# Eighteen gated pairs by seven block products, and state outputs as column halves

## The chip, the cores and the metric

The kernel runs on one core of a Trainium2 chip, as one launch. The metric is device time in microseconds (us), less is better; the time of a kernel is the median of its runs. Engines are named as in the profile: PE (TensorE, matmuls) with PEld (its weight loads), DVE (VectorE), ACT (ScalarE), POOL (GpSimd) and SP (SyncE, which issues most DMAs).

## What is computed

The kernel is a two-layer encoder trunk on 512 positions of width 1024, in float32. Layer 0 mixes positions by gated linear attention and a second recurrent mixer, layer 1 by retention and a diagonal complex state space (S5). After each mixer stands a gated feed-forward with a width-3 convolution over the positions:

```python
def conv_ffn(h, w_up, conv_w, conv_b, w_down):      # h: (1, 512, 1024), normed
    u = jnp.einsum('bsd,df->bsf', h, w_up)          # w_up: 1024 x 5632
    ...
    c = conv_b + up[:, 0:s] * conv_w[0]             # up: u padded by one position
    for t in range(1, CONV_WIDTH):
        c = c + up[:, t:t + s] * conv_w[t]
    a, v = jnp.split(c, 2, axis=-1)                 # 2816 columns each
    return jnp.einsum('bsf,fd->bsd', jax.nn.silu(a) * v, w_down)
...
x = x + conv_ffn(rmsnorm(x, g), ...)
```

The S5 part of layer 1 turns its states into outputs by matmuls with the real and the imaginary part of a matrix and a skip term.

## The kernel before, in words

Activations lie transposed: channels on the 128 partitions, the 512 positions along the free axis, so x is eight tiles of 128 x 512. Matmuls keep float32 precision by splitting both operands into a high part (a rounded copy, by ACT) and a low part (the rest, by DVE): `load_split` (L182, L184) does it for a weight chunk of 128 x 1024, `norm_split` for the activations. A product is then three matmuls, high x high, high x low, low x high (`mm3`). All matmuls go through the helper `mm`, so all have line L192.

The feed-forward (`ffn`) has 22 gated pairs. Pair m is two column blocks of 128, the gate m and the value m + 22. `up` makes each block from a weight chunk, with 8 x 3 matmuls of 512 columns (tile `pu`). `up_evac` scales the two results by the norm factor (`upad`, L306), convolves them (ACT starts `c` at L310, DVE adds two taps at L313), applies SiLU (`sa`, L318), multiplies (`g`, L320) and splits the product into `gh` (ACT, L323) and `gl` (DVE, L324). `down` multiplies a round of gated tiles by a down chunk into `pd` and adds the result to one tile of x (L346). ROUNDS sets three rounds of 8, 7 and 7 pairs: after the pairs of a round (and one more) come eight down products, one for each tile of x. The last three down products of the second feed-forward are made in column halves of 256 (`last`, tile `pl`), so that the final norm of the first half starts early.

The order of the work is set by a small scheduler in the program (`Sched`): it takes matmul jobs in the order of a list (`ffn_jobs`), issues the weight loads of the next three chunks ahead, and lets side chains advance when a clock of estimated matmul time has passed (the numbers in `W`). Each engine then runs its instructions in the order in which they stand; semaphores make the engines wait for each other. Weight chunks go through four raw buffers and four buffers each for the high and the low part.

In the S5 part, `states` makes the states' inputs `px` in column halves (two matmuls with 64 weight columns each, into partitions 0 to 63 and 64 to 127), and `outputs` makes `py` with three matmuls over 128 weight columns for each of four groups. It does so four times.

Of the kernel before, what the change touches and what calls it, by code (L numbers as in the profile page):

```python
# [11 lines left out]
F32 = mybir.dt.float32  # L12
F32R = mybir.dt.float32r
I32 = mybir.dt.int32
AF = mybir.ActivationFunctionType
# [28 lines left out]
ROUNDS = [list(range(0, 8)), list(range(8, 15)), list(range(15, 22))]  # L44
# [92 lines left out]
class Net:  # L137
# [33 lines left out]
    def load_raw(self, src, shape, name):  # L171
        n = int(np.prod(shape))
        raw = self.wp.tile([128, 1024], F32, tag="wraw", name=f"r_{name}", bufs=4)
        self.nc.sync.dma_start(out=raw[:, 0:n], in_=src)
        return raw, shape, name

    def load_split(self, raw, shape, name):
        nc = self.nc
        n = int(np.prod(shape))
        hi = self.wp.tile([128, 1024], F32R, tag="whi", name=f"h_{name}", bufs=4)  # L180
        lo = self.wp.tile([128, 1024], F32R, tag="wlo", name=f"l_{name}", bufs=4)
# [6 lines left out]
    def chunk(self, src, shape, name):  # L188
        return self.load_split(*self.load_raw(src, shape, name))

# [90 lines left out]
    def ffn(self, L, env, x, nxt, side=None, tail=None):  # L281
# [3 lines left out]
        with ExitStack() as st:  # L285
# [4 lines left out]
            gh, gl = {}, {}  # L290
            upad = []
            for i in range(4):
                u = fq.tile([128, S + 2], F32, tag=f"upad{i}", name=f"upad{L}_{i}")
                nc.gpsimd.memset(u[:, 0:1], 0.0)
                nc.gpsimd.memset(u[:, S + 1 : S + 2], 0.0)
                upad.append(u)
# [4 lines left out]
            def up_evac(m, pss):  # L301
                cs = []
                for half in range(2):
                    j = m + MF * half
                    u = upad[(2 * m + half) % 4]
                    nc.vector.tensor_tensor(  # L306
                        out=u[:, 1 : S + 1], in0=pss[half], in1=self.rbc, op=ALU.mult)
# [11 lines left out]
                g = fq.tile([128, S], F32, tag="g", name=f"g{L}_{m}", bufs=2)  # L319
                nc.vector.tensor_tensor(out=g, in0=sa, in1=cs[1], op=ALU.mult)  # L320
                h = fp.tile([128, S], F32R, tag="gh", name=f"gh{L}_{m}", bufs=9)
                l = fp.tile([128, S], F32R, tag="gl", name=f"gl{L}_{m}", bufs=9)
                nc.scalar.activation(h, g, AF.Copy)  # L323
                nc.vector.tensor_tensor(out=l, in0=g, in1=h.bitcast(F32), op=ALU.subtract)  # L324
                gh[m], gl[m] = h, l

# [8 lines left out]
            def down(r, ks, *chs):  # L335
                ms = ROUNDS[r]
# [8 lines left out]
                for k, ps in zip(ks, pd):  # L345
                    nc.vector.tensor_tensor(out=x[k], in0=ps, in1=x[k], op=ALU.add)  # L346
                    if r == len(ROUNDS) - 1:
                        nxt(k, x[k])

            def last(ks, *chs):  # L350
                ms = ROUNDS[-1]
# [13 lines left out]
            env.update(up=up, down=down, last=last)  # L365
# [6 lines left out]
    def ffn_jobs(self, L):  # L372
# [8 lines left out]
        done = -1  # L381
        for r, ms in enumerate(ROUNDS):
            upto = min(ms[-1] + 1, MF - 1)
            for m in range(done + 1, upto + 1):
                up(m)
            done = upto
            groups = [[k] for k in range(KD)]
            if r == len(ROUNDS) - 1:
                groups[0:2] = [[0, 1]]
                if L:  # L390
                    groups[-3:] = [[5, 6, 7]]
            for ks in groups:
                J(lambda *chs, r=r, ks=ks: env["down"](r, ks, *chs) if len(ks) < 3 else env["last"](ks, *chs),
                  [(self.I[f"w_down{L}_{r}"][k], (len(ms), 128), f"d{L}_{r}_{k}") for k in ks])
# [699 lines left out]
    def odd(self, env):  # L1094
# [50 lines left out]
        def s5():  # L1145
# [61 lines left out]
            def outputs(Q):  # L1207
                w1, w2, w0, E, H4 = st_.pop(Q)
# [248 lines left out]
    def start(self, warm):  # L1457
# [8 lines left out]
        raw += [self.wp.tile([128, 1024], F32, tag="wraw", name=f"r_qk{i}", bufs=4) for i in range(2)]  # L1466
# [227 lines left out]
```

## Time and profile before

| | |
|---|---|
| three runs, median | 1243.82 us (1243.2 to 1245.39) |
| the profiled execution, its own time | 1242.25 us |
| its span, first to last instruction | 1240.3 us |
| busy: PE / PEld | 99% / 82% |
| busy: DVE / ACT / POOL | 67% / 40% / 16% |
| mean granted TensorE clock | 0.996 of full speed |
| DMA | 133 MB, mean 107 GB/s |

Busy shares are averages over stages with different limits. The chain of waits follows the work that ended last back from the end: at each step to what released it, or to the instruction before it on its engine. A start in a timeline minus the start before it is the time that an instruction occupies its engine; the duration is a little longer, since neighbours overlap. "Idle before" is what an engine waited ahead of an instruction, with the one that released it.

### The profile page before, as it was taken

What the parts mean: (1) busy time and instruction counts of PE and PEld (TensorE: products, weight loads), DVE (VectorE), ACT (ScalarE), POOL (GpSimd) and SP (SyncE); (2) the same over time, 40 slices, a digit from 0 to 9 for tenths busy, and PEclk for the clock granted to TensorE, in tenths of its full rate; (3) what the DMA queues carried; (4) which work ended last, traced back from release to release, by engine and by line L of the source; (5) the groups of instructions that cost most, each with busy time, mean ns of one, the idle gap of its engine ahead of it and who ended that gap; (6) DMA issues with size and microseconds to landing.
All of it is one profiled execution on the core that took longest, in us unless ns stands there. A gap on an engine that the chain in (4) does not pass through costs nothing.

```text
span 1240.3 us, 19118 instructions
## 1 busy us (share of the span) xinstructions
PE 1224.3 (99%) x7675; PEld 1019.1 (82%) x7675; DVE 836.8 (67%) x1315; ACT 497.0 (40%) x659; POOL 195.4 (16%) x279
## 2 busy tenths in 40 slices
PE   9999999999999999999999998999999999999997
PEld 7788878888888888888889897888888888888886
DVE  6668766569985688567657866756677547745753
ACT  6545344344443444244433244325444224423442
POOL 1000001050084463500122320003000000000012
PEclk9999999999999999999999999999999999999999
DMA  7132132232316234342456533123233222233211
GB/s 246 49 104 69 36 121 86 78 127 86 98 39 192 88 121 143 123 159 71 153 169 203 166 98 125 62 85 119 86 102 102 87 101 100 83 107 102 91 45 68
DMA packets 54504, 133.01 MB, mean 107 GB/s; under 512 B 12432, under 2 KB 17936, under 8 KB 54416
## 3 DMA queue, kind: packets, MB, share of 16 engines
q1 hardware_dynamic: 53696, 131.25, 32.0%
q8 instruction: 60, 0.98, 0.3%
q10 hardware_dynamic: 720, 0.55, 0.1%
q14 instruction: 28, 0.23, 0.1%
HBM read 120.24 MB, written 11.53 MB: 106 GB/s over the span
## 4 chain that ended last, share of the span: by engine, by line
PE 94%; DVE 3%; issue 1%; POOL 1%; ACT 0%; DMA 0%; POOLq 0%; SPq 0%; DVEq 0%; ACTq 0%
PE pu L192 39%; PE pd L192 18%; PE wo L192 6%; PE v L192 4%; PE p_g L192 4%; PE sc L192 2%; PE ov L192 2%; PE p_q L192 2%; PE p_k L192 2%; PE p_hz L192 2%; PE p_rg L192 2%; PE pl L192 1%; PE rv L192 1%; PE o L192 1%; PE p_hq L192 1%
## 5 line engine op out<-in xcount | busy, mean ns | idle before, releaser
L192 PE MATMUL pu<-xh_f,h_u 128*128 128x512 f32 x704 | 275.2, 391 | 0.0
L192 PE MATMUL pu<-xh_f,l_u 128*128 128x512 f32 x704 | 274.1, 389 | 0.0
L192 PE MATMUL pu<-xl_f,h_u 128*128 128x512 f32 x704 | 274.1, 389 | 0.0
L192 PEld LDWEIGHTS pu<-xh_f,h_u 128*128 128x128 f32 x704 | 132.2, 188 | 28.3 <-issue 1.2
L192 PEld LDWEIGHTS pu<-xh_f,l_u 128*128 128x128 f32 x704 | 132.1, 188 | 27.8
L192 PEld LDWEIGHTS pu<-xl_f,h_u 128*128 128x128 f32 x704 | 132.2, 188 | 27.1
L182 ACT ACTIVATE h_u<-r_u 128x1024 fp32r<-128x1024 f32 x88 | 93.1, 1058 | 117.3 <-PE pd L192 52.8
L313 DVE SCALAR_TENSOR_TENSOR c<-upad,convp,c 128x512 f32<-128x512 f32 x176 | 133.5, 760 | 3.8 <-ACT c L310 1.0
L192 PE MATMUL pd<-gh,h_d 128*128 128x512 f32 x331 | 129.3, 391 | 0.0
L192 PE MATMUL pd<-gh,l_d 128*128 128x512 f32 x331 | 128.9, 389 | 0.0
L192 PE MATMUL pd<-gl,h_d 128*128 128x512 f32 x331 | 128.9, 389 | 0.0
L184 DVE TENSOR_TENSOR l_u<-r_u,h_u 128x1024 fp32r<-128x1024 f32 x88 | 108.8, 1236 | 16.2 <-ACT h_u L182 15.6
L306 DVE TENSOR_TENSOR upad<-pu,rstd_f 128x512 f32<-128x512 f32 x88 | 60.5, 688 | 71.1 <-PE pu L192 69.5
L346 DVE TENSOR_TENSOR x<-pd,x 128x512 f32<-128x512 f32 x45 | 31.0, 690 | 90.3 <-PE pd L192 90.3
L310 ACT ACTIVATE c<-upad,convp 128x512 f32<-128x512 f32 x88 | 71.3, 811 | 20.0 <-DVE upad L306 17.2
L323 ACT ACTIVATE gh<-g 128x512 fp32r<-128x512 f32 x44 | 27.8, 632 | 113.8 <-DVE g L320 113.8
L192 PEld LDWEIGHTS pd<-gh,l_d 128*128 128x128 f32 x331 | 62.1, 188 | 13.1
L192 PEld LDWEIGHTS pd<-gh,h_d 128*128 128x128 f32 x331 | 62.1, 188 | 13.1 <-issue 0.4
L192 PEld LDWEIGHTS pd<-gl,h_d 128*128 128x128 f32 x331 | 62.2, 188 | 12.8
L182 ACT ACTIVATE h_d<-r_d 128x896 fp32r<-128x896 f32 (+1 forms) x48 | 47.2, 987 | 63.4 <-PE pd L192 42.2
L318 ACT ACTIVATE sa<-c 128x512 f32<-128x512 f32 x44 | 27.8, 632 | 81.1 <-DVE c L313 81.1
L184 DVE TENSOR_TENSOR l_d<-r_d,h_d 128x896 fp32r<-128x896 f32 (+1 forms) x48 | 55.0, 1147 | 6.6 <-ACT h_d L182 4.4
(418 smaller groups left out, 2273.9 us busy)
## 6 DMA issues: line engine op xcount, KB each, us to landing
r_u<-in_w_up SPq DMA_DIRECT2D x88, 512.0 KB, 3.5
r_d<-in_w_down SPq DMA_DIRECT2D x32, 448.0 KB, 3.4
r_wo<-in_w_out SPq DMA_DIRECT2D x16, 512.0 KB, 3.4
r_d<-in_w_down SPq DMA_DIRECT2D x16, 512.0 KB, 3.5
w<-dw SPq DMA_DIRECT2D x20, 256.0 KB, 4.9
r_v<-in_we_v SPq DMA_DIRECT2D x8, 512.0 KB, 3.8
r_g<-in_we_g SPq DMA_DIRECT2D x8, 512.0 KB, 3.8
r_ov<-in_wo_v SPq DMA_DIRECT2D x8, 384.0 KB, 3.6
```

The lines of the kernel that those rows point to most:

```text
L182: nc.scalar.activation(hi[:, 0:n], raw[:, 0:n], AF.Copy)
L184: eng.tensor_tensor(out=lo[:, 0:n], in0=raw[:, 0:n], in1=hi[:, 0:n].bitcast(F32), op=ALU.subtract)
L192: self.nc.tensor.matmul(ps, a, b, start=start, stop=stop)
L306: nc.vector.tensor_tensor(out=u[:, 1 : S + 1], in0=pss[half], in1=self.rbc, op=ALU.mult)
L310: nc.scalar.activation(c, u[:, 1 : S + 1], AF.Identity, scale=cw[:, 1:2], bias=cw[:, 3:4])
L313: nc.vector.scalar_tensor_tensor(out=c, in0=u[:, o : o + S], scalar=cw[:, tap : tap + 1], in1=c, op0=ALU.mult, op1=ALU.add)
L318: nc.scalar.activation(sa, cs[0], AF.Silu)
L323: nc.scalar.activation(h, g, AF.Copy)
L346: nc.vector.tensor_tensor(out=x[k], in0=ps, in1=x[k], op=ALU.add)
```

## The change

Pairs 4 to 21 of the second feed-forward (18 of 22) are made by Strassen's scheme in its form with seven products. For a pair the weights are seen as two by two blocks: gate and value columns by the upper and the lower half of the input channels. The activations are two by two as well: lower and upper half of the channels by the first and the second 256 positions. Seven block products of 128 columns by 512 channels by 256 positions replace eight.

- `right` makes the seven right operands once, from the normed activations (tiles `bh`, `bl`, four of 128 x 1792 each): DVE normalises, POOL forms four differences, ACT and DVE split. It waits for the norm factor.
- `block_loads` makes the weight side of a pair: the two loaded chunks, two chunks of sums and differences (tiles `ws`, four 512-wide additions on POOL), and the splits: `ua`, `us`, `ut` of 1024 columns and `ug` of 512.
- `blocks` runs the products, two in a PSUM tile `pb`, and puts them together in `upad` by five additions on DVE, two copies on ACT and one addition on POOL (on DVE for the last pair). `gated` is the rest of the old evacuation; the product `g` now overwrites `sa`.
- The rounds of the second feed-forward become 4 ordinary pairs and 6, 6 and 6 changed ones, and the eight down products of a round are put between the blocks of the next round, four for every three pairs. `gh` and `gl` of most changed pairs take over the buffers of the normed activations.
- Raw, high and low weight buffers go from four to five, and loads are issued four chunks ahead in the second feed-forward.
- `py` is made in column halves: six matmuls with 64 weight columns for each group.

The diff, cut to its core:

```diff
+M0 = 4
+cut = lambda *e: [list(range(i, j)) for i, j in zip((0,) + e, e)]
-ROUNDS = [list(range(0, 8)), list(range(8, 15)), list(range(15, 22))]
+ROUNDS = [cut(8, 15, 22), cut(M0, 10, 16, 22)]
...
+        def split(r, n, w=1024):
+            hi, lo = (self.wp.tile([128, 1024], F32R, tag=t, name=f"{t[1]}_{n}{L}_{m}", bufs=5)
+                      for t in ("whi", "wlo"))
+            nc.scalar.activation(hi[:, 0:w], r, AF.Copy)
+            nc.vector.tensor_tensor(
+                out=lo[:, 0:w], in0=r, in1=hi[:, 0:w].bitcast(F32), op=ALU.subtract)
...
+        def sums():
+            a, g = raw
+            p, q = (self.sums.tile([128, 1024], F32, tag="ws", name=f"s{i}{L}_{m}", bufs=2)
+                    for i in range(2))
+            tt(p[:, H], g[:, E], g[:, H], ALU.add)
+            tt(p[:, E], p[:, H], a[:, E], ALU.subtract)
+            tt(q[:, E], a[:, E], g[:, E], ALU.subtract)
+            tt(q[:, H], a[:, H], p[:, E], ALU.subtract)
+            ws.append(q)
+            return split(p, "us")
+
+        fns = (straight, sums, lambda: split(ws[0], "ut"), lambda: split(raw[1][:, H], "ug", 512))
...
+            def right():
+                yield (lambda: self.rbc is not None), 0.0
...
+                    for o, p, q in ((c(0), x2, x1), (c(2), y2, x2), (c(1), y2, c(0)), (c(3), y1, c(1))):
+                        gp.tensor_tensor(out=o, in0=p, in1=q, op=ALU.subtract)
+                    for e, f in ((slice(0, n), x1), (slice(n, 3 * n), xb), (slice(3 * n, 7 * n), s)):
+                        nc.scalar.activation(bh[:, e], f, AF.Copy)
+                        nc.vector.tensor_tensor(
+                            out=bl[:, e], in0=f, in1=bh[:, e].bitcast(F32), op=ALU.subtract)
...
+            def product(ps, ch, part, slot):
+                for k in range(4):
+                    w = (ch[0][:, 4 * part + k, :], ch[1][:, 4 * part + k, :])
+                    e = slice(256 * slot, 256 * slot + 256)
+                    self.mm3(ps, w, (BH[k][:, e], BL[k][:, e]), k == 0, k == 3)
+                    yield
+
+            def blocks(m, i, ch):
...
+                if i == 0:
+                    yield from product(ps[:, h0], ch, 0, 0)
+                    nc.scalar.activation(u[:, 1, lf], ps[:, h0], AF.Copy)
+                    yield from product(ps[:, h1], ch, 1, 1)
+                    add(u[:, 0, lf], ps[:, h1], u[:, 1, lf])
+                elif i == 1:
+                    un = fq.tile([128, 2, 256], F32, tag="un", name=f"un{L}_{m}", bufs=1)
+                    UN[m] = un
+                    yield from product(ps[:, h0], ch, 0, 4)
+                    add(un[:, 0], ps[:, h0], u[:, 1, lf])
+                    yield from product(ps[:, h1], ch, 1, 3)
+                    P5[m] = ps[:, h1]
+                elif i == 2:
+                    un = UN[m]
+                    yield from product(ps[:, h0], ch, 0, 5)
+                    add(un[:, 1], ps[:, h0], un[:, 0])
+                    add(u[:, :, rt], un, P5.pop(m).unsqueeze(1).to_broadcast([128, 2, 256]))
+                    yield from product(ps[:, h1], ch, 1, 2)
+                    add(u[:, 0, rt], ps[:, h1], u[:, 0, rt])
+                else:
+                    un = UN.pop(m)
+                    yield from product(ps[:, h0], ch, 0, 6)
+                    if m == MF - 1:
+                        add(u[:, 1, lf], ps[:, h0], un[:, 1])
+                    else:
+                        nc.scalar.activation(u[:, 1, lf], ps[:, h0], AF.Copy)
+                        add(u[:, 1, lf], u[:, 1, lf], un[:, 1], nc.gpsimd)
+                    gated(m)
...
+            for r, ms in enumerate(ROUNDS[L][1:]):
+                before = downs(r)
+                for m in ms:
+                    for i, loads in enumerate(self.block_loads(L, m)):
+                        J(lambda ch, m=m, i=i: env["blocks"](m, i, ch), loads,
+                          lambda: len(env["BL"]) == 4)
+                        if (4 * m + i) % 3 == 1:
+                            next(before, None)
...
-                    self.mm(py[:, g, :], w0[:, c], ug, True, False)
-                    self.mm(py[:, g, :], w2[0][:, c], H4[:, 0, g, :], False, False)
-                    self.mm(py[:, g, :], w2[1][:, c], H4[:, 1, g, :], False, True)
+                    for i, (w, y) in enumerate(
+                            ((w0, ug), (w2[0], H4[:, 0, g, :]), (w2[1], H4[:, 1, g, :]))):
+                        for h in heads:
+                            self.mm(py[h, g, :], w[:, c][:, h], y, i == 0, i == 2, cost=57)
```

The order of the instructions, at two places. First DVE in the second feed-forward, a pair in the middle of the stage (the first number behind a name is the pair, for `upad` the buffer; the last number is the program's own; `l_` are low parts of weights, of an up or a down chunk). Before, pair 10, with the splits for pair 12 between:

```order
L306 TENSOR_TENSOR upad_0_8362<-pu_10_0_9452,rstd_f_8435 128x512
L184 TENSOR_TENSOR l_u_12_0_9480<-r_u_12_0_9477,h_u_12_0_9479 128x1024
L313 SCALAR_TENSOR_TENSOR c_10_0_9509<-upad_0_8362,convp,c_10_0_9509 128x512 x2
L306 TENSOR_TENSOR upad_1_8365<-pu_10_1_9483,rstd_f_8435 128x512
L184 TENSOR_TENSOR l_u_12_1_9529<-r_u_12_1_9526,h_u_12_1_9528 128x1024
L313 SCALAR_TENSOR_TENSOR c_10_1_9514<-upad_1_8365,convp,c_10_1_9514 128x512 x2
L320 TENSOR_TENSOR g_10_9520<-sa_10_9518,c_10_1_9514 128x512
L324 TENSOR_TENSOR gl_10_9523<-g_10_9520,gh_10_9522 128x512
```

Now, from the third block of pair 6 on, with the splits for pair 7 and a down split between:

```order
L208 TENSOR_TENSOR l_us_7_9227<-s_7_9220,h_us_7_9226 128x1024
L420 TENSOR_TENSOR un_6_9174<-pb_6_2_9230,un_6_9174 128x256
L420 TENSOR_TENSOR upad_0_8382<-un_6_9174,pb_6_1_9173 128x2x256
L420 TENSOR_TENSOR upad_0_8382<-pb_6_2_9230,upad_0_8382 128x256
L208 TENSOR_TENSOR l_ut_7_9259<-s_7_9221,h_ut_7_9258 128x1024
L359 SCALAR_TENSOR_TENSOR c_6_0_9277<-upad_0_8382,convp,c_6_0_9277 128x512
L208 TENSOR_TENSOR l_ug_7_9293<-r_u_7_1_9167,h_ug_7_9292 128x512
L359 SCALAR_TENSOR_TENSOR c_6_0_9277<-upad_0_8382,convp,c_6_0_9277 128x512
L359 SCALAR_TENSOR_TENSOR c_6_1_9281<-upad_0_8382,convp,c_6_1_9281 128x512 x2
L420 TENSOR_TENSOR upad_1_8385<-pb_7_0_9296,upad_1_8385 128x256
L366 TENSOR_TENSOR sa_6_9285<-sa_6_9285,c_6_1_9281 128x512
L187 TENSOR_TENSOR l_d_0_5_9326<-r_d_0_5_9323,h_d_0_5_9325 128x512
```

The splits of a pair now stand among the additions and taps of the pair before it, and a down split, before in a stretch of its own, among them.

Second POOL, from the norm of the second feed-forward to the end of the stage. Before, the clearing of the padding (`upad`) and the norm factor (`ncol_f`) are followed by the sums of the final norm (`nacc_fin`):

```order
L294 MEMSET upad_3_8371 128x1
L295 MEMSET upad_3_8371 128x1
L252 TENSOR_TENSOR ncol_f_8408<-nvar_f_8407,mhalf 128x4
L222 TENSOR_TENSOR nacc_fin<-nacc_fin,nsq_fin_10699 128x512
L222 TENSOR_TENSOR nacc_fin<-nacc_fin,nsq_fin_10732 128x512
```

Now the weight sums stand there (`s`, of pairs 7 and 8 here), and the last addition of a pair (L420) among the sums for the pair after next:

```order
L202 TENSOR_TENSOR s_7_9220<-s_7_9220,r_u_7_0_9165 128x512
L202 TENSOR_TENSOR s_7_9221<-r_u_7_0_9165,r_u_7_1_9167 128x512
L420 TENSOR_TENSOR upad_1_8385<-upad_1_8385,un_5_9016 128x256
L202 TENSOR_TENSOR s_7_9221<-r_u_7_0_9165,s_7_9220 128x512
L202 TENSOR_TENSOR s_8_9378<-r_u_8_1_9345 128x512
L202 TENSOR_TENSOR s_8_9378<-s_8_9378,r_u_8_0_9343 128x512
L420 TENSOR_TENSOR upad_0_8382<-upad_0_8382,un_6_9174 128x256
```

POOL, idle through the stage before, now works in it on sums for the pair after the one that DVE puts together, with that pair's last addition in their queue.

## Rows read from the trace of the kernel before

**Rows 1.** The page, busy us and share of the span by engine, then instructions
```profile
PE 1224.3 (99%) x7675; PEld 1019.1 (82%) x7675; DVE 836.8 (67%) x1315; ACT 497.0 (40%) x659; POOL 195.4 (16%) x279
```

**Rows 2.** Chain of waits, 1010 to 1190 us: start us, us, what
```profile
1010.65 76.16 PE pu L192 x336
1086.81 38.08 PE pd L192 x168
```

**Rows 3.** Busy us (instructions) by engine, 1011 to 1087 us: second feed-forward, ordinary pairs
```profile
core 0: us, PE busy (x) PEld busy (x) DVE busy (x) ACT busy (x) POOL busy (x), PEclk, DMA share, GB/s
1011.00:1087.00 76.00, 76.00 (x337) 62.95 (x336) 52.46 (x67) 32.48 (x41) 0.00 (x0) 1.00 0.28 91
```

**Rows 4.** Chain of waits, 1213 to 1231 us, the last group's column halves
```profile
1213.97 9.35 PE pl L192 x78
```

**Rows 5.** Timeline of PE, second state outputs: start us, us, engine, line, operation
```profile
688.99 0.33 PE L192 MATMUL py<-U,w 128*128 128x64 f32 x2
...
691.90 1.15 PE L192 MATMUL px<-U,w 128*64 128x64 f32 x32
692.98 0.36 PE L192 MATMUL rv<-ovh,rAh 128*128 128x192 f32 x1
```

**Rows 6.** Chain of waits, odd layer, 674 to 727 us
```profile
674.58 2.62 PE py L192 x24
...
686.76 7.22 issue
...
713.12 1.22 PE rs L192 x3
...
723.86 2.62 PE py L192 x24
```

**Rows 7.** Timeline of DVE, 879 to 889 us, second feed-forward
```profile
879.82 0.75 DVE L313 SCALAR_TENSOR_TENSOR c<-upad,convp,c 128x512 f32<-128x512 f32 x1
880.49 0.69 DVE L306 TENSOR_TENSOR upad<-pu,rstd_f 128x512 f32<-128x512 f32 x1
...
885.93 0.69 DVE L306 TENSOR_TENSOR upad<-pu,rstd_f 128x512 f32<-128x512 f32 x1
886.53 1.21 DVE L184 TENSOR_TENSOR l_u<-r_u,h_u 128x1024 fp32r<-128x1024 f32 x1
887.67 1.60 DVE L313 SCALAR_TENSOR_TENSOR c<-upad,convp,c 128x512 f32<-128x512 f32 x2
```

**Rows 8.** Timeline of DVE, 1226 to 1229 us, the end
```profile
1227.30 1.41 DVE L1569 TENSOR_TENSOR x<-x,bc_fin 128x256 f32<-128x256 f32 x4
```

**Rows 9.** Timeline of DVE, 248 us, before the first feed-forward
```profile
248.11 3.48 DVE L234 SCALAR_TENSOR_TENSOR xl_f<-x,gains,xh_f 128x512 fp32r<-128x512 f32 x2
```

**Rows 10.** Timeline of POOL, the same place
```profile
247.88 3.16 POOL L222 TENSOR_TENSOR nacc_f<-nacc_f,nsq_f 128x512 f32<-128x512 f32 x2 [0.87 <-ACT nsq_f L220]
```

**Rows 11.** Timeline of DVE, 869 us, with POOL at rest
```profile
869.37 0.75 DVE L234 SCALAR_TENSOR_TENSOR xl_f<-x,gains,xh_f 128x512 fp32r<-128x512 f32 x1
```

**Rows 12.** Timeline of POOL, 1227 us, the end
```profile
1226.94 2.13 POOL L1567 TENSOR_TENSOR x<-x,rstd_fin 128x256 f32<-128x256 f32 x3 [1.85 <-ACT rstd_fin L1563]
```

**Rows 13.** Groups, 1011 to 1087 us: busy us, mean ns, idle before, releaser
```profile
L182 ACT ACTIVATE h_u<-r_u 128x1024 fp32r<-128x1024 f32 x11 | 11.7, 1062 | 14.9 <-PE pu L192 10.6 <-PE pd L192 4.4
L306 DVE TENSOR_TENSOR upad<-pu,rstd_f 128x512 f32<-128x512 f32 x14 | 9.7, 690 | 16.8 <-PE pu L192 16.8
L324 DVE TENSOR_TENSOR gl<-g,gh 128x512 fp32r<-128x512 f32 x6 | 4.2, 692 | 4.2 <-ACT gh L323 4.2
```

**Rows 14.** Timeline of ACT, 877 us, the norm factor
```profile
876.69 0.60 ACT L268 ACTIVATE rstd_f<-bc_f 128x512 f32<-128x512 f32 x1 [2.13 <-PE bc_f L192]
```

**Rows 15.** Chain of waits, 867 to 968 us, start of the second feed-forward
```profile
867.33 4.76 PE pu L192 x21
872.87 2.89 PE pu L192 x12
...
876.65 90.48 PE pu L192 x399
```

More of the change, by code (lines that the diff above doesn't have):

```diff
@@ L290, in ffn @@
             gh, gl = {}, {}
+            BH, BL, UN, P5 = [], [], {}, {}
             upad = []
[L292 to L295, printed above, removed]
+            for i in range(2):
+                u = fq.tile([128, 2, S + 2], F32, tag=f"upad{i}", name=f"upad{L}_{i}")
+                nc.gpsimd.memset(u[:, :, 0:1], 0.0)
+                nc.gpsimd.memset(u[:, :, S + 1 : S + 2], 0.0)
                 upad.append(u)
@@ L301, in up_evac, with gated @@
             def up_evac(m, pss):
+                for half in range(2):
+                    nc.vector.tensor_tensor(
+                        out=upad[m % 2][:, half, 1 : S + 1], in0=pss[half], in1=self.rbc,
+                        op=ALU.mult)
+                gated(m)
+            def gated(m):
                 cs = []
@@ L304, in up_evac @@
                     j = m + MF * half
-                    u = upad[(2 * m + half) % 4]
-                    nc.vector.tensor_tensor(
-                        out=u[:, 1 : S + 1], in0=pss[half], in1=self.rbc, op=ALU.mult)
+                    u = upad[m % 2][:, half, :]
                     c = fq.tile([128, S], F32, tag=f"c{half}", name=f"c{L}_{m}_{half}", bufs=2)
@@ L364, in ffn @@
             pss = {}
-            env.update(up=up, down=down, last=last)
+            env.update(up=up, down=down, last=last, blocks=blocks, BL=BL)
+            if L:
+                self.sch.ahead, self.sums = 4, fp
+                self.sch.chain(right())
             self.sch.chain(self.norm_end(lambda n: new_ps("sm", n, 1), W[f"f{L}_bc"]), W[f"f{L}_cs"])
@@ L379, in up, with downs @@
                   [(self.I[f"w_up{L}"][m, half], (KD, 128), f"u{L}_{m}_{half}")])
[L381 to L384, printed above, removed]
-                up(m)
[L386 to L394, printed above, removed]
+        def downs(r):
+            ms = ROUNDS[L][r]
+            groups = [[k] for k in range(KD)]
+            if r == len(ROUNDS[L]) - 1:
+                if L:
+                    groups = [[0, 1, 2], [3], [4], [5, 6, 7]]
+                else:
+                    groups[0:2] = [[0, 1]]
+            for i, ks in enumerate(groups):
+                J(lambda *chs, i=i, ks=ks: env["last"](ks, *chs) if i and len(ks) > 1 else
+                  env["down"](r, ks, *chs),
+                  [(self.I[f"w_down{L}_{r}"][k], (len(ms), 128), f"d{L}_{r}_{k}") for k in ks])
+                yield
+        if not L:
+            done = -1
+            for r, ms in enumerate(ROUNDS[L]):
+                upto = min(ms[-1] + 1, MF - 1)
+                for m in range(done + 1, upto + 1):
+                    up(m)
+                done = upto
+                for _ in downs(r):
+                    pass
+        else:
+            for m in ROUNDS[L][0]:
+                up(m)
+            for r, ms in enumerate(ROUNDS[L][1:]):
[6 more added lines that the diff above has]
+                            next(before, None)
+                for _ in before:
+                    pass
+            for _ in downs(r + 1):
+                pass
         self.sch.barrier()
@@ L1465, in start @@
         raw = [self.load_raw(self.I["we_lr"], (KD, 32), "lr")[0]]
-        raw += [self.wp.tile([128, 1024], F32, tag="wraw", name=f"r_qk{i}", bufs=4) for i in range(2)]
+        raw += [self.wp.tile([128, 1024], F32, tag="wraw", name=f"r_qk{i}", bufs=5) for i in range(2)]
         xs = {}
```

70 lines of the change are left out of this document (57 added, 13 removed), and 2 rows, old and new, of the table W.

## Prediction

> **What bounds the kernel now.** I read the busy line first, then the chain of waits, then the stage that changes, engine by engine. TensorE (PE) is busy 1224.3 of 1240.3 us [rows 1], but matmul ends are modelled there, so that alone proves little. The chain says more: through the second feed-forward it holds nothing but matmuls, 336 of the up projection in 76.16 us and 168 of the down projection in 38.08 us [rows 2]. So one 512-wide matmul costs 76.16/336 = 226.7 ns with its weight load hidden, and a gated pair (2 chunks x 8 x 3 = 48 matmuls) costs 10.88 us. VectorE (DVE) does 52.46 us in 76.00 there, GpSimd (POOL) nothing [rows 3]. The stage is PE bound, with a third of DVE and all of POOL free. The change spends both to take matmuls away, so the question is whether they suffice.
>
> **Part 1, matmuls saved.** A changed pair has 7 products x 4 x 3 = 84 matmuls of 256 columns. The kernel already has that width at its end: 78 matmuls `pl` in 9.35 us, 119.9 ns each [rows 4], more than half of 226.7. A pair is 10.07 us, 0.81 less; 18 pairs give **-14.6 us**. The down products are as many as before (22 x 8 x 3). Of the last group 108 matmuls are narrow instead of 126: 18 x 119.9 against 9 x 226.7 ns, -0.1 us.
>
> **Part 2, state outputs.** The outputs `py` go from 24 matmul records a group over 128 columns of weights to 48 over 64, in two halves that can lie beside each other. `px` stands in that form already: its 32 records pass in 692.98 - 691.90 = 1.08 us, 34 ns each, where the 24 of `py` take 691.90 - 688.99 = 2.91 us [rows 5]; elsewhere 2.62 [rows 6]. 48 x 34 ns = 1.63 us, so about 1.0 us less for each of four groups. But between 686.76 and 713 us the chain runs over POOL, DVE and issue, not PE [rows 6]; two groups stand on the chain (674.58, 723.86). I take **-2.1 us**, from 0 (all covered) to -4.3.
>
> **Part 3, what DVE gets.** Prices are from start to start, since DVE overlaps neighbours: 512-wide 0.60 us (885.93 to 886.53), 1024-wide 1.14 (886.53 to 887.67), a convolution tap 0.67 (879.82 to 880.49) up to 0.80 where two on one tile follow each other [rows 7]; 256-wide from PSUM 0.33 to 0.35 (four in 1.41) [rows 8]. A changed pair has three splits of 1024 and one of 512 (4.0), five additions that put the seven products together (four of 256, one of 512: 1.9), four taps (2.9), and `g` and `gl` (1.2): 10.0 us. The scaling by the norm, 2 x 0.60, is gone. To each pair come 4/3 down jobs, each a split and an addition to x: with four parts 0.60 + 0.60, with six some 0.87 (estimated between the 512 and 1024 prices) + 0.60. That makes 11.6 us a pair in the first round of blocks (pairs 4 to 9, downs of four) and 12.0 in the next two (pairs 10 to 21, downs of six). PE needs 10.07 + 4/3 x 12 x 0.2267 = 13.70 and 10.07 + 4/3 x 18 x 0.2267 = 15.51 us. Alone, DVE would fit.
>
> **Part 4, what POOL takes from DVE.** Each changed pair puts four 512-wide additions of weights and one 256-wide on POOL. The trace shows what happens when both engines read two operands from SBUF: two `xl_f` together took 3.48 us while two POOL additions `nacc_f` ran [rows 9, 10]; without POOL one lasts 0.75 [rows 11] and two would take 0.67 + 0.75. So a 512-wide POOL instruction met head-on costs DVE (3.48 - 1.42)/2 = 1.03 us. For one of 256, which lasts 2.13/3 = 0.71 us on POOL [rows 12], I take half, some 0.53. DVE instructions that read PSUM are not held: four in 1.41 us beside three POOL ones [rows 8, 12]. Met head-on throughout, a pair loses 4 x 1.03 + 0.53 = 4.7 us; at best nothing. In DVE's order the first weight sum of the next pair is released by `l_us`, and three PSUM additions follow there, which cover it; the second meets `l_ut` with some 0.8 left; the third and fourth, released by `l_ut`, meet taps and splits, 1.0 each; the 256-wide one falls where DVE waits for `c` in any case. That is **2.8 us** a pair, my value, between 0 and 4.7. In-order waits come on top: `gl` waited 4.2 us in six pairs for ACT's `gh` [rows 13], 0.7 each; the new order puts another row between in most pairs, so I take 0.4.
>
> The Trainium skill, "SBUF — State Buffer", section "SBUF: two separate sides", has the rule: the port pair that DVE and GpSimd share is an exclusive lock for DVE instructions with two SBUF inputs, and whoever starts first holds it for the whole instruction. By that rule the trace agrees (3.48 us for two where 0.75 is one's own), and the rule speaks against this change, whose relief for DVE runs on the engine that locks it out; taken to its end it gives rival A.
>
> So DVE needs 11.6 + 2.8 + 0.4 = 14.8 us a pair in the first round against PE's 13.70: 1.1 x 6 = **+6.6 us**. In the other two it needs 15.2 against 15.51: nothing.
>
> **Part 5, the start.** The blocks need the seven right operands, which wait for the norm factor `rstd_f` (ends at 877.3 us [rows 14]). PE does its four ordinary pairs by 876.65 + 159 x 0.2268 = 912.7 us [rows 15] and wants the second block tile 2.9 us later, at 915.6. By then DVE has: eight products 5.4, their splits 4 x 2.07 = 8.3, the evacuation of pairs 0 and 1 (2 x 5.3), the scaling of pair 2 (1.2), four weight splits (4.6), one of a down (0.6): 30.7 us. POOL's sixteen 256-wide and four 512-wide instructions cost it, at the same share as above (2.8/4.7 = 0.6), 0.6 x (16 x 0.53 + 4 x 1.03) = 7.6. 877.3 + 38.3 = 915.6, just in time with no wait at all; for waits on ACT and POOL I take **+3 us**, 0 to 8.
>
> What I cost at nothing: ACT, 32.48/7 = 4.6 us an ordinary pair [rows 3], gets 1.5 splits of 1.06 us more [rows 13], two short copies and 4/3 down splits, some 8.3 a pair, hidden under PE; weight loads by DMA, as many bytes a pair as before at a 0.28 DMA share [rows 3]; the fifth weight buffer. At the very end 45 down matmuls (10.2 us) cover the last pair's evacuation.
>
> **Sum.** 1242.25 (the profiled execution, span 1240.3) - 14.6 - 0.1 - 2.1 + 6.6 + 3 = 1235.0. That execution lies 1.6 us below the median of the runs, 1243.82, so I predict a median of **1236.6 us**. About 0.2% (2.5 us) is what a measurement can tell: faster is below 1241.3, slower above 1246.3.
>
> **Rivals.**
> *A, POOL locks DVE out.* If the loss is 4.0 of 4.7 us a pair, because DVE is always backed up and every weight sum meets a split or a tap, DVE needs 16.0 and 16.4 us: +2.3 x 6 + 0.9 x 12 = 24.6, with 6 at the start 30.6, against 16.8 gained: **1257.6 us**, slower. It decides from about 3.3 us a pair: 6 x 1.6 + 12 x 0.2 + 5 = 17. For it: both `xl_f` of [rows 9] lost the full price, and some 11 of a pair's 18 DVE rows read SBUF twice. Against it: DVE stalls for PE results between, and a POOL instruction then costs nothing. Chance 0.28.
> *B, POOL hides.* If its instructions fall into DVE's waits for PE, DVE fits under PE everywhere: 1242.25 - 16.8 + 1.6 = **1227 us**. For it: `upad` waited 16.8 us for PE in seven pairs [rows 13]. Against it: that idle third is what the change fills. Chance 0.22.
> *C, late gated values.* Each round's first down product follows one block tile (2.9 us) behind the last pair of its round, and its last part comes 9 or 15 x 0.227 = 2.0 or 3.4 us on; so the chain behind the last product (ACT copy, POOL, ACT, two taps, `g`, `gh`, `gl`: by the prices above about 5 us unqueued) is given 4.9 or 6.3. Queued on a full DVE it is 2 us late at three boundaries, over my forecast: **1242.6 us**, no change. Chance 0.13.
> *D, the saving is not there.* At 129.5 ns for 256 columns (226.7 x 48/84) the products save nothing, and it is 1251 us; the 78 `pl` speak against it. Chance 0.04.
> My forecast has 0.33; most of it, and B, lie on the fast side.
>
> **Numbers.** Faster 0.56 (B, the forecast but for its upper edge, a little of C), same 0.13, slower 0.31 (A, D). The forecast's own range is 1231 to 1243. The range for 8 in 10 runs from 1225 (B with all four `py` counted) to 1260 (past the centre of A; the full 4.7 us and more waits would give 1280, and are left out).
>
> **What would show it.** Right: `pb` matmuls near 119.9 ns apart; DVE above nine tenths between 913 and 995 us, with PE stalls there released by `l_` splits; taps and splits whose mean grows by some 0.2 us; POOL busy 6 to 7 us a pair. A would show PE waiting for `l_us` and `l_ut` in all three rounds and taps near 1.2 us on average; B, PE without gaps and DVE waiting for `pb`; C, PE waiting on `gl` at `pd` alone. I am wrong if `pb` costs over 125 ns, or if the stalls come from ACT or DMA.

## The result, and the profile after

The changed kernel takes 1352.44 us (median of 4 runs, 1349.76 to 1353.9), the kernel before, beside it, 1243.51 us. The ratio is 1.0875 (95% interval 1.0847 to 1.0902): 109 us slower, where 7 us faster was forecast. The profiled execution has a span of 1349.3 us.

The page first: busy us and share of the span by engine. It is the line that answers to [rows 1].

```profile
PE 1237.0 (92%) x8410; PEld 1050.4 (78%) x8410; DVE 938.5 (70%) x1442; ACT 541.6 (40%) x750; POOL 330.1 (24%) x376
```

No engine is full any more. PE was at 99% and is at 92%, DVE rose only from 67% to 70%. So nothing became a new bound; the engines wait for each other. Where they do is told by the busy time by stretch, second feed-forward and end (the columns are those of [rows 3]):

```profile
core 0: us, PE busy (x) PEld busy (x) DVE busy (x) ACT busy (x) POOL busy (x), PEclk, DMA share, GB/s
627.00:869.00 242.00, 235.70 (x1466) 202.22 (x1465) 168.99 (x272) 86.82 (x119) 42.49 (x45) 0.99 0.41 132
...
916.00:1035.00 119.00, 83.80 (x504) 76.74 (x504) 83.24 (x102) 43.78 (x65) 40.73 (x31) 0.83 0.22 66
1035.00:1165.00 130.00, 102.14 (x655) 92.20 (x656) 87.87 (x109) 49.23 (x70) 40.53 (x31) 0.97 0.24 76
1165.00:1297.00 132.00, 105.81 (x682) 95.12 (x682) 88.57 (x111) 50.36 (x71) 34.22 (x26) 0.98 0.23 72
```

From 627 to 869 us, the odd layer, PE is idle for 6.3 us, little more than before the change (5.8 in 627 to 867). From 916 to 1297, where the changed pairs run, it is idle for 89 of 381 us, DVE is busy for 259.68 of 381 (68%), and the granted clock, 1.00 in the second feed-forward before [rows 3], is 0.83, 0.97 and 0.98. The waits of PE from 912 to 1300 us say for whom (us in total, times, longest us):

```profile
PE pb L232 <- ACT upad L424: 49.2, 18, 17.2
PE pb L232 <- DVE un L420: 42.2, 35, 2.8
PE pd L232 <- ACT gh L376: 1.5, 2, 0.7
PE pd L232 <- DVE gl L377: 0.6, 2, 0.3
```

The block products `pb` wait 18 times for an ACT copy and 35 times for a DVE addition `un`. There are 18 changed pairs, and each has three PSUM tiles that hold two products: one whose first half is read by the copy, two whose first half is read by `un`. So PE waits at each of these 54 tiles (the last one falls behind 1300 us), 91.4 us in 53 places, and hardly anywhere else. One such place in the timeline of PE (start us, us, engine, line, operation, idle before it and what ended that); the rows left out are more matmuls of the same products and of the first one on the next tile:

```profile
1061.35 0.28 PE L232 MATMUL pb<-bh,h_us 128*128 128x256 f32 x1
1061.47 0.28 PE L232 MATMUL pb<-bl,h_us 128*128 128x256 f32 x1
...
1062.67 0.28 PE L232 MATMUL pb<-bh,l_us 128*128 128x256 f32 x1
1064.08 0.39 PE L232 MATMUL pb<-bh,h_us 128*128 128x256 f32 x1 [1.13 <-DVE un L420]
1064.30 0.28 PE L232 MATMUL pb<-bl,h_us 128*128 128x256 f32 x1
...
1066.93 0.28 PE L232 MATMUL pb<-bh,l_ut 128*128 128x256 f32 x1
1068.46 0.39 PE L232 MATMUL pb<-bh,h_ut 128*128 128x256 f32 x1 [1.25 <-DVE un L420]
```

And the timeline of DVE at the same place:

```profile
1062.46 1.23 DVE L208 TENSOR_TENSOR l_ua<-r_u,h_ua 128x1024 fp32r<-128x1024 f32 x1 [0.22 <-ACT h_ua L207]
1063.61 0.42 DVE L420 TENSOR_TENSOR un<-pb,upad 128x256 f32<-128x256 f32 x1
```

The first product's twelve matmuls follow each other at 0.12 us, as forecast. The last ends at 1062.95. Its result is read by `un`, which stands in DVE's queue behind a split and ends at 1064.03; the first matmul of the second product starts at 1064.08. All its operands were there: it uses the same weight chunk. What it waits for is `un`, which reads the other half of the tile that it writes.

The largest single wait, 17.18 us, is the first of its kind. The timeline of PE and of ACT at the first changed pair:

```profile
928.88 0.58 PE L232 MATMUL pb<-bh,h_ua 128*128 128x256 f32 x1 [17.18 <-ACT upad L424]
929.26 0.42 PE L232 MATMUL pb<-bl,h_ua 128*128 128x256 f32 x1
929.48 0.42 PE L232 MATMUL pb<-bh,l_ua 128*128 128x256 f32 x1
```

```profile
913.50 1.06 ACT L207 ACTIVATE h_us<-s 128x1024 fp32r<-128x1024 f32 x1 [4.42 <-POOL s L202]
...
920.44 1.06 ACT L207 ACTIVATE h_ut<-s 128x1024 fp32r<-128x1024 f32 x1 [3.52 <-POOL s L202]
...
928.47 0.36 ACT L424 ACTIVATE upad<-pb 128x256 f32<-128x256 f32 x1
```

The copy takes 0.36 us, but in ACT's order it stands behind splits that wait for POOL's weight sums and gating steps that wait for DVE. The product that it releases runs at 1.2 GHz, the lower clock level (granted clock 0.50 in 917 to 935 us), with 0.21 us from matmul to matmul instead of 0.12.

An account by PE, in spans: 1240.3 us before, less the 14.6, 0.1 and 2.1 us that the forecast saves on PE, is 1223.5. The waits above come to 93.5 us. The lower clock is, by an estimate from the three stretches (busy time x what is missing from 1.00), 83.80 x 0.17 + 102.14 x 0.03 + 105.81 x 0.02 = 19.4 us. Counted in the timeline instead, 142 of the block matmuls went at 0.21 us and not at 0.12, some 13 us, so that the estimate is rather high. With the estimate the sum is 1336 of the 1349.3 us. Most of the rest stands at the same waits: at 1064.08 the profile counts 1.13 us as idle, but the starts before and behind it, 1062.67 and 1064.30, lie 1.63 us apart where two steps of 0.12 would do. That is 1.39 us lost, 0.26 more than counted, and 53 times 0.26 is 14 us. So the account closes to within 6 us.

### The profile page after: what moved, and what is told of

The parts are those of the page before. It is cut to its first block, busy times and chain, and to the rows that moved or that the text cites. A ratio compares the mean times of both kernels' runs of the same rounds, so it can differ in the third digit from the quotient of the medians.

```text
span 1349.3 us, 21087 instructions
## 1 busy us (share of the span) xinstructions
PE 1237.0 (92%) x8410; PEld 1050.4 (78%) x8410; DVE 938.5 (70%) x1442; ACT 541.6 (40%) x750; POOL 330.1 (24%) x376
## 3 DMA queue, kind: packets, MB, share of 16 engines
q8 instruction: 66, 1.08, 0.3%
## 5 line engine op out<-in xcount | busy, mean ns | idle before, releaser
L232 PE MATMUL pu<-xh_f,h_u 128*128 128x512 f32 x416 | 163.2, 392 | 0.0
L232 PE MATMUL pu<-xh_f,l_u 128*128 128x512 f32 x416 | 162.1, 390 | 0.0
L232 PE MATMUL pu<-xl_f,h_u 128*128 128x512 f32 x416 | 162.1, 390 | 0.0
L232 PE MATMUL pb<-bh,h_ua 128*128 128x256 f32 x144 | 45.2, 314 | 50.5 <-ACT upad L424 49.2
L232 PEld LDWEIGHTS pu<-xh_f,h_u 128*128 128x128 f32 x416 | 78.1, 188 | 17.1 <-issue 1.2
L232 PEld LDWEIGHTS pu<-xh_f,l_u 128*128 128x128 f32 x416 | 78.1, 188 | 16.4
L232 PEld LDWEIGHTS pu<-xl_f,h_u 128*128 128x128 f32 x416 | 78.2, 188 | 15.9
L187 DVE TENSOR_TENSOR l_d<-r_d,h_d 128x768 fp32r<-128x768 f32 (+3 forms) x56 | 65.6, 1173 | 22.1 <-ACT h_d L185 21.3
L185 ACT ACTIVATE h_d<-r_d 128x768 fp32r<-128x768 f32 (+3 forms) x56 | 48.5, 871 | 71.2 <-PE pb L232 24.2
L187 DVE TENSOR_TENSOR l_u<-r_u,h_u 128x1024 fp32r<-128x1024 f32 x52 | 65.5, 1260 | 9.8 <-ACT h_u L185 9.5
L202 POOL TENSOR_TENSOR s<-r_u 128x512 f32<-128x512 f32 x18 | 23.6, 1310 | 191.5 <-DVE l_us L208 191.4
```

Source lines behind the costliest of these rows:

```text
L185: nc.scalar.activation(hi[:, 0:n], raw[:, 0:n], AF.Copy)
L187: eng.tensor_tensor(out=lo[:, 0:n], in0=raw[:, 0:n], in1=hi[:, 0:n].bitcast(F32), op=ALU.subtract)
L202: tt = lambda o, x, y, op: G.tensor_tensor(out=o, in0=x, in1=y, op=op)
L232: self.nc.tensor.matmul(ps, a, b, start=start, stop=stop)
```

## The experiments

My theory after this (T1) was the shared tile. Its main rivals were rival A of the prediction, POOL's port (T2), and a clock that falls by itself (T3).

### 1. Reads behind both products

```diff
                     yield from product(ps[:, h0], ch, 0, 0)
-                    nc.scalar.activation(u[:, 1, lf], ps[:, h0], AF.Copy)
                     yield from product(ps[:, h1], ch, 1, 1)
+                    nc.scalar.activation(u[:, 1, lf], ps[:, h0], AF.Copy)
...
-                    add(un[:, 0], ps[:, h0], u[:, 1, lf])
                     yield from product(ps[:, h1], ch, 1, 3)
+                    add(un[:, 0], ps[:, h0], u[:, 1, lf])
```

The third tile of a pair is altered in the same way.

> The changed kernel with one thing altered: of the two block products that share a PSUM tile, the reads of the first half are issued after the matmuls of the second, so that the second product no longer has to wait for them. Nothing else moves. Theory T1 (the two products of a tile are serialised by the tile, and the gaps, 93 us of TensorE's idle time between 912 and 1300, also pull the clock down): the waits of pb on upad (49.2 us) and un (42.2 us) fall below 20 us together, most of what is left standing at the start of the first changed pairs, the granted clock of 935 to 1297 goes back to 0.98 or more, and the time to 1240 to 1265. Theory T2 (POOL's sums hold VectorE off the shared port, and TensorE waits for late split chunks): the time stays above 1310, with pb now waiting for l_us, l_ut and l_ug. Theory T3 (the clock alone: the 256-column products themselves let it fall): the waits go, but the slow stretches stay, time 1275 to 1310.

Measured: 1271.2 us, 81 us less than the change; ratio to the kernel before 1.0228 (1.0213 to 1.0244). The largest waits of PE from 866 to 1310 us:

```profile
PE pd L232 <- ACT gh L376: 31.9, 4, 11.7
PE pb L232 <- DVE upad L344: 1.3, 1, 1.3
PE pb L232 <- ACT h_d L185: 1.1, 1, 1.1
```

The waits on `un` and on the copy are gone, and 1040 to 1090 us now reads (columns as above)

```profile
1040.00:1090.00 50.00, 50.00 (x351) 46.98 (x350) 45.78 (x56) 25.67 (x36) 22.17 (x16) 1.00 0.29 93
```

with PE full at clock 1.00. That bears T1 out and drops T3 as a cause of its own: the 256-column products held the full clock here, where they follow each other. One sign of T1 did not come, and the time lies 6 us above what it expected: the clock is still 0.90 in 990 to 1040 and 0.93 in 1090 to 1140 us. There a wait that had been hidden came out: the first down products of each round now wait for `gh`.

### 2. No weight sums on POOL

```diff
             a, g = raw
-            p, q = (self.sums.tile([128, 1024], F32, tag="ws", name=f"s{i}{L}_{m}", bufs=2)
-                    for i in range(2))
...
-            ws.append(q)
-            return split(p, "us")
+            ws.append(a)
+            return split(g, "us")
```

> The changed kernel without POOL's four weight sums of a pair: the chunks are split as they come (the product of the second tile takes the g chunk and that of the third the a chunk, so that another product is computed). POOL's sums of the right operand and the additions for the convolution stay, and so do the shared PSUM tiles. T1 (shared tile): nearly all of the 35 waits on un and most of those on upad stay, about 1.2 us each; only part of the 17.2 us at the start and of the wait for late chunks goes: 1305 to 1340. T2 (POOL and the port): VectorE's splits go back to about 1.2 us, the waits go, and the time falls to 1235 to 1270.

Measured: 1324.1 us, 28 us less than the change and inside what T1 expected. The largest waits of PE from 866 to 1310 us:

```profile
PE pb L226 <- DVE un L414: 46.5, 36, 1.8
PE pb L226 <- ACT upad L418: 29.0, 18, 11.2
```

The 54 waits stay without any of POOL's weight sums. T2 falls as the main cause.

### 3. Both edits

Experiments 1 and 2 together.

> Both of the two edits before: reads of a shared tile after both of its products, and no weight sums on POOL (another product is computed, as in the run without sums). It gives what POOL's sums cost once the shared tile is out of the way: the difference to the run with the first edit alone. T1: 2 to 15 us less than that run, the most of it at the start of the changed pairs; the sum of the prediction without its lock term is near 1230. T2: over 40 us less than that run.

Measured: 1246.0 us (ratio 1.0027, 1.0016 to 1.0038), 25 us less than experiment 1 and 78 less than 2. The four kernels form a square: the shared tile costs 81 us with POOL's sums and 78 without; the sums cost 28 us with the shared tile and 25 without. The two causes add up. The 25 us are above the 2 to 15 that I expected: POOL's sums cost more than the start alone. And the 1230 that the expectation names for the prediction without its lock is missed by 16 us; PE still waits 12.6 us for `gh` here.

### 4. The column halves alone

The kernel before, with `py` alone altered as in the change's diff.

> The kernel before with only the state outputs as two column halves of 64. The prediction gave this part 2.1 us (0 to 4.3). In the trace of the change py ends 3.4 us earlier than in that of before although it starts 0.9 us later, so about 4 us is expected by that: 1238 to 1240.5 against 1243.5. If the edit is worth nothing by itself, the time is within 0.2% of before.

Measured: 1241.07 us against 1242.85 beside it, ratio 0.9982 (0.9973 to 0.9991), that is -2.2 us (-3.4 to -1.1; the two medians lie 1.8 us apart). In the chain of waits a group now takes (answering to [rows 6])

```profile
674.76 1.55 PE py L192 x48
```

instead of 2.62 us. My expectation, 3 to 5.5 us less, was too much: it put the whole shift of `py` in the trace of the change down to this edit, and the weight buffers are others there too.

### 5. The down products later

Experiment 1, with

```diff
-                        if (4 * m + i) % 3 == 1:
+                        t, n = 4 * (m - ms[0]) + i, 4 * len(ms) - 1
+                        if t in [5 + (n - 5) * k // 7 for k in range(8)]:
                             next(before, None)
```

> The run with both products ahead of the reads, with one thing more: the first down product of a round comes behind the sixth tile of the next round's pairs instead of behind the first, and the eight are spread over the rest. In that run TensorE waited 31.9 us in four places for gh, all at the first down products of a round (11.65 and 5.25 at 914 to 934, 9.13 at 1022.6, 5.82 at 1128.1), and the clock fell behind each. Theory L (these waits are only the latency of the gating of the round's last pair, with one tile of 2.9 us to cover it): the waits for gh at 1022 and 1128 go, that at the start shrinks and turns into a wait for the split weight sums of the first pair, and the time is 1238 to 1255. Theory D (VectorE, 92% busy in 1040 to 1090 with POOL's port behind it, has fallen behind TensorE and the lost time comes back wherever the next wait is): the waits reappear at other tiles, 1262 to 1275.

Measured: 1254.9 us, 16 us less than experiment 1, at the upper edge of theory L. Both theories hold a part. The waits for `gh` are gone; PE's largest waits from 866 to 1310 us are

```profile
PE pb L232 <- DVE upad L344: 9.6, 2, 5.6
PE pb L232 <- DVE upad L420: 7.6, 4, 3.6
```

so PE now waits for DVE's evacuations. DVE is busy for 52.68 of 55 us in 935 to 990. It has fallen behind, and about half of the 31.9 us comes back in another place.

### 6. The right operand earlier

Experiment 5 with `"right": 4500.0`.

> The run with the later down products, and the right operand prepared faster: the step between its four parts at 4500 instead of 6500 units of the program's own count. In the changed kernel the last part's differences and the first pair's weight sums meet on POOL at 908 to 914, and ScalarE's queue waits for them. If the stall at 910 to 930 is that meeting, 3 to 10 us less than the run with the later down products alone: 1232 to 1250. If VectorE has no room before 908 (it is 77% busy in 869 to 916), no change or up to 4 us more.

Measured: 1254.9 us, no difference to experiment 5. PE's wait for `upad` of the ordinary pairs only changes its form, from 9.6 us in two places to 6.9 in one, while that for the `upad` of the blocks (L420) grows from 7.6 to 11.0. The second expectation holds.

### 7. The weight sums on VectorE

```diff
-        tt = lambda o, x, y, op: G.tensor_tensor(out=o, in0=x, in1=y, op=op)
+        tt = lambda o, x, y, op: nc.vector.tensor_tensor(out=o, in0=x, in1=y, op=op)
```

on experiment 1.

> The run with both products ahead of the reads, with the four weight sums of a pair on VectorE instead of POOL (the lock by POOL's sums goes, VectorE has four 128x512 additions more a pair, 0.68 to 0.75 us each by the rows of other such operations, 2.7 to 3.0 us a pair). The prediction put the lock at 2.8 us a pair (0 to 4.7). If that is right VectorE's busy time with its waits hardly changes and the time is 1255 to 1275, the most of a gain at the start, where a sum then takes 0.7 instead of 1.3 to 1.7 us. If the lock is worth nothing in the sum, VectorE is over TensorE and the time is 1275 to 1310.

Measured: 1254.2 us, 17 us less than experiment 1, just past the fast end of what I expected. DVE's busy time in 1040 to 1090 us is 47.67 us; with the sums on POOL it was 45.78, and 40.37 with none (experiment 3). In that stretch the sums cost DVE 5.41 us when POOL makes them and 7.30 when DVE makes them itself. So POOL takes little of the work off DVE (the three stretches don't hold quite the same instructions; the groups of the next section are the cleaner measure). And a sum takes POOL 1.3 to 1.7 us (908 to 944 us in experiment 1), DVE 0.69. The waits of `pd` for `gh` fall from 31.9 to 17.2 us.

### 8. Experiments 5, 6 and 7 together

> All of these together: both products ahead of the reads, later down products, the right operand at 4500, the weight sums on VectorE. By theory L and a lock worth 2.8 us a pair: 1230 to 1250, within 8 us of the same without the sums on VectorE. If VectorE is then the bound: over 1255.

Measured: 1242.7 us, ratio 0.9994 (0.9983 to 1.0005): level with the kernel before, and 12.2 us less than experiment 6, where I had allowed 8. The largest wait of PE that is left is at the start, 7.47 us from 910 us on for `upad` of the ordinary pairs.

### 9. The differences of the right operand on VectorE too

```diff
-                        gp.tensor_tensor(out=o, in0=p, in1=q, op=ALU.subtract)
+                        nc.vector.tensor_tensor(out=o, in0=p, in1=q, op=ALU.subtract)
```

on experiment 8.

> The last run (both products ahead of the reads, later down products, the right operand at 4500, weight sums on VectorE) with the sixteen differences of the right operand on VectorE too, 0.42 us each by the rows of 256-wide operations there, 6.7 us in all. In the trace of the last run each of the four parts of the right operand waited 3.1 to 6.0 us on POOL between xb and the split of t, with ScalarE's and VectorE's queues standing behind it, and TensorE then waited 7.5 us at 910 for upad of the ordinary pairs. If the loss at 910 to 935 is that detour: the wait of 7.5 us shrinks below 3 and the time is 1230 to 1240. If it is VectorE's own backlog (it is busy for 23.00 of 23 us in 912 to 935): 1240 to 1247.

Measured: **1236.41 us** against 1243.73, ratio 0.9941 (0.9928 to 0.9953): faster than both kernels, by 7.3 and 116 us. The wait at 910 us is gone; PE's longest from 866 to 1310 us are

```profile
PE pb L232 <- ACT upad L447: 4.1, 2, 2.1
PE pu L232 <- DVE upad L344: 1.5, 1, 1.5
PE pb L232 <- DVE upad L420: 1.4, 1, 1.4
```

### 10. The same, with the right operand at 3000

> As the run with the differences on VectorE, with the right operand's step at 3000 instead of 4500 units, so that its four parts come earlier among the ordinary pairs, where VectorE has idle time (14.5 of 45 us in 867 to 912). If the backlog is a matter of when it is built up: 2 to 6 us less than that run. If the earlier parts only push the evacuations of the first ordinary pairs back: 0 to 5 us more.

Measured: 1236.5 us, no difference. The pace of the right operand is not what decides.

### 11. The shared tile back in the fastest version

Experiment 9 without the edit of experiment 1.

> The fastest version (reads of a tile behind both of its products, later down products, weight sums and differences on VectorE, 1236.4) with the first of these edits taken back: the reads of the first half stand again ahead of the second product. If the shared tile costs by itself what it cost in the changed kernel, 70 to 90 us come back: 1305 to 1325, with some 54 waits of pb of 1.1 to 1.7 us for un and upad and the granted clock below 1.0 behind them. If the tile only cost so much because POOL's sums kept VectorE late with the reads, under 1290.

Measured: 1319.8 us, 83 us more than experiment 9. The largest waits of PE from 866 to 1310 us:

```profile
PE pb L232 <- DVE un L420: 51.5, 36, 7.2
PE pb L232 <- ACT upad L424: 20.2, 18, 3.6
```

On POOL only one 256-wide addition a pair is left that could hold DVE up, and the 54 waits are back, with the clock at 0.70 in 912 to 935 us and at 0.97 to 1.00 behind. The shared tile costs about 80 us in each of the three surroundings that were tried.

### 12. The fastest version without the column halves

> The fastest version without the column halves of the state outputs. Alone these gave 1.8 us in the ratio (0.9982, interval 0.9973 to 0.9991). If the two parts of the change add up: 1237.5 to 1240.5, that is, Strassen's products with the waits taken out are worth 3 to 6 us against the kernel before; if the odd layer's gain is used up elsewhere, 1236 to 1237.

Measured: 1237.89 us, ratio 0.9957 (0.9945 to 0.9969). So the seven products, once they run without these waits, are worth 4.8 us against the 1242.71 beside them. The rest of Part 1's 14.6 us is not in it: in this run PE still waits 7.6 us for `upad` and `gh` at five places of the second feed-forward, with a clock of 0.93 behind the first ones, and the kernel before has no such waits. With the 0.9982 of experiment 4 that multiplies to 0.9939, where 0.9941 was measured: the two parts of the change add up.

## Why the prediction was wrong

**The step that failed is Part 1, "A pair is 10.07 us".** The price of a matmul was right (0.12 us apart, so rival D is out). What failed is that the 84 were taken to follow each other. The change puts two products in one PSUM tile and reads the first before it starts the second, and PE waits for that read, 91.4 us in 53 places: 5.1 us a pair, against 0.81 saved. I costed the five additions and the two copies as work of DVE and ACT and never asked what PE does between the halves. Two things could have shown it. The change's own code has the read between the two products. And the `pl` of [rows 4] are halves of one tile too: there three tiles are gone through before the second halves begin, so their reads are covered, and I took 119.9 ns from a place where the wait could not show. Of the signs that I had named for being right, two did not come: DVE is busy for 83.24 of 119 us (916 to 1035) where I expected over nine tenths, and no split releases PE.

The Trainium skill has the rule, in "PSUM — Partial Sum Buffer", section "PSUM bank collisions raise a hardware error": two engines may not touch the same bank in the same partitions at once, whichever addresses of it they use, so whatever schedules the program has to keep them apart. The trace agrees as far as it goes: the second half's matmul starts 0.05 us after the read of the first has ended. By the rule half-bank tiles would not have helped. No run here tried tiles of their own for the two products, so it stays open whether the chip needs this wait or only the program's way of ordering accesses to one tile; that the wait is the loss is shown by experiments 1, 3 and 11.

**The clock** was not in the prediction at all. In the first 119 us of the changed pairs it was granted at 0.83; most of the 13 to 19 us that it cost were lost there. It followed the gaps: with the gaps taken out (experiment 9) the profile shows 1.00 from 935 to 1190 us.

**Part 2 was right:** -2.1 us forecast, -2.2 us measured (experiment 4), with the two groups on the chain that it counted.

**Parts 3 and 4, DVE and POOL, were near in what DVE loses, but not in what follows from it.** DVE's groups show what the lock costs. Experiment 1, sums on POOL, 950 to 1190 us (count, busy us, mean ns, idle before):

```profile
L359 DVE SCALAR_TENSOR_TENSOR c<-upad,convp,c 128x512 f32<-128x512 f32 x59 | 62.0, 1084 | 13.8 <-ACT c L356 13.6
L208 DVE TENSOR_TENSOR l_ut<-s,h_ut 128x1024 fp32r<-128x1024 f32 x14 | 22.6, 1614 | 0.4 <-ACT h_ut L207 0.4
L187 DVE TENSOR_TENSOR l_d<-r_d,h_d 128x768 fp32r<-128x768 f32 (+1 forms) x19 | 22.0, 1155 | 0.0
...
L208 DVE TENSOR_TENSOR l_us<-s,h_us 128x1024 fp32r<-128x1024 f32 x14 | 17.0, 1213 | 1.2 <-ACT h_us L207 1.2
L208 DVE TENSOR_TENSOR l_ug<-r_u,h_ug 128x512 fp32r<-128x512 f32 x15 | 16.2, 1079 | 0.0
```

Experiment 9, sums on DVE, the same stretch:

```profile
L359 DVE SCALAR_TENSOR_TENSOR c<-upad,convp,c 128x512 f32<-128x512 f32 x64 | 45.5, 755 | 3.9 <-ACT c L356 3.8
L187 DVE TENSOR_TENSOR l_d<-r_d,h_d 128x768 fp32r<-128x768 f32 (+1 forms) x26 | 23.5, 905 | 0.4 <-ACT h_d L185 0.4
L208 DVE TENSOR_TENSOR l_ut<-s,h_ut 128x1024 fp32r<-128x1024 f32 x15 | 18.4, 1228 | 0.0
L208 DVE TENSOR_TENSOR l_us<-s,h_us 128x1024 fp32r<-128x1024 f32 x15 | 18.4, 1225 | 1.6 <-ACT h_us L207 1.4
...
L208 DVE TENSOR_TENSOR l_ug<-r_u,h_ug 128x512 fp32r<-128x512 f32 x15 | 10.7, 716 | 0.0
...
L202 DVE TENSOR_TENSOR s<-r_u 128x512 f32<-128x512 f32 x15 | 10.3, 689 | 1.2 <-DMA r_u<-in_w_up 1.0
```

A pair's four taps grow by 4 x 0.329 us, `l_ut` by 0.386, `l_ug` by 0.363, the 4/3 down splits by some 0.250 each (their mix of widths differs a little); `l_us` does not. That is 2.4 us a pair, against 2.8 forecast, and on the instructions that Part 4 named (`l_ut`, taps, splits). The sums themselves cost DVE 4 x 0.69 = 2.76 us. So the trade is nearly even. The lock itself shows where a split meets a sum, in the timelines of POOL and DVE in experiment 1:

```profile
922.16 1.59 POOL L202 TENSOR_TENSOR s<-s,r_u 128x512 f32<-128x512 f32 x1
922.55 2.28 DVE L208 TENSOR_TENSOR l_ut<-s,h_ut 128x1024 fp32r<-128x1024 f32 x1
```

The split ends 1.08 us after the sum has ended (924.83 and 923.75), near the 1.14 us that Part 3 has for such a split. The Trainium skill ("SBUF — State Buffer", section "SBUF: two separate sides") has this rule, an exclusive lock that the first to start holds for its whole instruction, and the two rows agree with it.

The 6.6 us of Part 4, DVE behind PE in the first round, did not show: in experiment 1 PE is busy for all of 950 to 990 us, with DVE at 37.89 of 40. What Part 4 did not see is that POOL is also late: each sum, at 1.3 to 1.7 us, holds up ACT's and DVE's queues. Experiments 3 and 7 put that whole detour at 17 to 25 us; that the sums' length is the reason is argued from the rows, not shown by a run of its own.

**Part 5, the start, was too small:** +3 us forecast (0 to 8). With the tile out of the way PE still waited 11.65 and 5.25 us at 914 to 934 us, and in 910 to 950 the clock was granted at 0.71 and 0.78. ACT's queue stood behind POOL's sums and differences. With both on DVE and the down products later (experiment 9) the waits at 915 to 927 us are 0.64, 1.38 and 1.96 us, which is about the size that Part 5 took.

**The rivals.** B is out, since POOL's weight sums cost 25 us (experiment 3). A is out as the cause: PE never waited for `l_us` or `l_ut` in the changed kernel, DVE was 68% busy, and without the sums 81 of 109 us stayed. Its slower time rested on DVE as the bound. C had the right place, the first down products of a round, but stayed hidden behind the tile waits: in the changed kernel `pd` waits 2.1 us in all, in experiment 1 it waits 32.

Experiment 9 lands at the forecast 1236.6 us. That is a coincidence and does not make the forecast right: it is another kernel, in which the tile waits and POOL's lock are taken away and the work of the sums is put on DVE.

## What to carry to other kernels

When several short products share a PSUM tile, put every read behind the last product that writes it, and let the next tile's matmuls cover the reads; a read between two products cost TensorE 42.2/35 = 1.2 us each time for `un`, and the clock on top. Price a change by what TensorE waits for between its matmuls, not by the engines' busy time alone: here 5.1 us of waits a pair, most of them small, outweighed a saving of 0.81 by far. A wait that is removed uncovers the next one, so a place where a product follows its operands closely (the down products here) is worth moving before it shows.

## What the runs showed of the hardware that was not expected

Giving work to an idle GpSimd and not to VectorE gained nothing: 2.4 us of delay on VectorE's other instructions for 2.76 us of sums, and putting the sums on VectorE made the kernel 17 us faster. VectorE's instructions that read PSUM were not delayed in it (`un` lasts 0.41 us on average in experiment 1, with POOL's sums, and 0.42 in experiment 9, without).

The clock fell behind the longest waits, not behind every one. In the changed kernel the timeline of PE has nine stretches in which the matmuls run at the lower level, the block matmuls 0.21 us apart, and each begins shortly behind one of the ten waits of 2.1 us or more; behind the 44 shorter waits, 0.5 to 1.6 us, none begins. That is no fixed limit: in experiment 9 the clock fell behind a wait of 1.96 us. On average that reads 0.97 and 0.98 over the 262 us from 1035 to 1297, while in experiment 1, with these waits gone, 1040 to 1090 us had 1.00. Behind its two longest waits, 11.65 and 5.25 us, experiment 1 had 0.71 in 910 to 930 us and 0.78 in 930 to 950.
